# A batched matmul on one core: the last stores on another queue, one of them split, x loaded earlier, transposes moved to their own batch

## The chip, the cores and the metric

The kernel runs on one core of a Trainium2 chip. The metric is the device time of one execution in microseconds (us), lower is better. The first six runs of the kernel before lie within 1.6 us (516.54 to 518.18 us, 0.3%), so differences of about 1 us need several runs, and here they also need the traces.

## The reference

```python
batch, m, k, n = 32, 512, 1024, 768
x:      float32 [32, 512, 1024]
weight: float32 [32, 1024, 768]
return np.matmul(x, weight).astype(np.float32)      # [32, 512, 768]
```

## The kernel before

For every batch, x (2 MB in HBM) and the weights (3 MB) are loaded on POOL's queue and cast to bf16 on the way; PE transposes x with an identity, multiplies, ACT and DVE copy the result out of PSUM, and the output (1.5 MB) is stored as a transfer of 128 partitions with a row of 12,288 bytes each. The last four batches go through their weights in chunks (`CHUNKED`), and in them the transposes of the next batch stand before the last chunk of the current one. Cuts are marked; the comments in the code are mine.

```python
CHUNKED = {B - 4: (4, 4), B - 3: (4, 4), B - 2: (4, 4), B - 1: (4, 2, 2)}
AHEAD = 3
# ... [cut] ...
x_pool = ctx.enter_context(tc.tile_pool(name="x", bufs=4))
# ... [cut] ...
for b in range(1, AHEAD):
    load_x(b)                      # nc.gpsimd.dma_start
    load_w(b)                      # nc.gpsimd.dma_start, one per chunk
ready = {}
for b in range(B):
    if b + AHEAD < B:
        load_x(b + AHEAD)
        load_w(b + AHEAD)
    if b > 0:
        nc.gpsimd.dma_start(out=out_view[b - 1], in_=outs[b - 1])
    outs[b] = out_pool.tile([P, MT * N], F32, name="out_sb")
    # ... [cut: batches that are not chunked] ...
    xT = ready.pop(b, None) or {mt: transpose(b, mt) for mt in range(MT)}
    pms = [banks() for _ in range(2)]
    at = 0
    for n in CHUNKED[b]:
        last = at + n == KT
        for mt in range(MT):
            if last and b + 1 < B:
                ready.setdefault(b + 1, {})[mt] = transpose(b + 1, mt)
            matmuls(pms[mt // 2], mt % 2, xT[mt], b, range(at, at + n), True)
            if last and mt % 2 == 1:
                pair = mt // 2
                evacuate(b, pair, pms[pair])
                if b == B - 1:     # the last output, two halves
                    cols = slice(pair * N2, (pair + 1) * N2)
                    nc.sync.dma_start(out_view[b, :, cols], outs[b][:, cols])
        at += n
```

## Time and profile before

| | before |
|---|---|
| median of the first 3 runs | 516.96 us (516.54 to 517.15) |
| span of the profiled run | 516.0 us |
| HBM traffic | 167.8 MB read, 50.3 MB written, 423 GB/s over the span |
| chain of waits | DMA 88%, PE 9% |

These are lines of the profile page of the kernel before: the DMA queues (packets, megabytes, share of the sixteen engines' span) and the summary of the chain that ended last.

```profile
q0 software_dynamic: 14256, 131.60, 98.9%
q1 hardware_dynamic: 432, 3.67, 1.9%
q8 instruction: 20, 0.33, 0.2%
...
HBM read 167.77 MB, written 50.33 MB: 423 GB/s over the span
...
DMA 88%; PE 9%; issue 1%; DVE 0%; ACT 0%; POOLq 0%
```

Queue 0 is POOL's, queue 1 SP's, and queue 8 brings instructions: 20 packets of 16 KB. The kernel is bound by DMA. The next view is the table by stages of the kernel before, 1 us each, at its end. Its last three columns are the granted TensorE clock, the mean busy share of the DMA engines and the GB/s that they moved.

```profile
core 0: us, PE busy (x) PEld busy (x) DVE busy (x) ACT busy (x) POOL busy (x), PEclk, DMA share, GB/s
505.00:506.00 1.00, 1.00 (x8) 0.59 (x7) 0.00 (x0) 0.00 (x0) 0.00 (x0) 1.00 0.90 381
506.00:507.00 1.00, 1.00 (x8) 0.67 (x7) 0.00 (x0) 0.44 (x1) 0.00 (x0) 1.00 0.60 258
507.00:508.00 1.00, 1.00 (x8) 0.59 (x6) 0.69 (x1) 0.87 (x3) 0.00 (x0) 1.00 0.43 184
508.00:509.00 1.00, 0.54 (x3) 0.10 (x1) 0.64 (x1) 0.83 (x2) 0.00 (x0) 1.00 0.46 190
509.00:510.00 1.00, 0.00 (x0) 0.00 (x0) 0.05 (x1) 0.16 (x1) 0.00 (x0) 1.00 1.01 418
510.00:511.00 1.00, 0.00 (x0) 0.00 (x0) 0.00 (x0) 0.00 (x0) 0.00 (x0) 1.00 1.01 412
511.00:512.00 1.00, 0.00 (x0) 0.00 (x0) 0.00 (x0) 0.00 (x0) 0.00 (x0) 1.00 1.02 418
```

The dip at 506 to 509 us looks like 1.5 us of DMA time lost to waiting for PE. And a store transfer of 128 partitions alone, at a share of 1.01 to 1.02, moves 412 to 418 GB/s; this pair of numbers, share against GB/s, will matter.

Why the dip is not lost time is seen in what the page averages away. The trace has sixteen completion marks for each of these transfers. I read them as one for each DMA engine. For the last weights and the transfers after them in the kernel before, in us:

| transfer | first mark | last mark | last mark after the one before it |
|---|---|---|---|
| last weights of batch 31 | 491.07 | 496.45 | |
| store 27 | 494.88 | 500.12 | 3.67 |
| store 28 | 498.60 | 503.80 | 3.68 |
| store 29 | 502.26 | 507.45 | 3.65 |
| store 30 | 505.91 | 511.11 | 3.66 |
| store 31, first half | 511.00 | 512.97 | 1.86 |
| store 31, second half | 512.89 | 514.80 | 1.83 |

The slowest engine goes on without a hole: every 1.5 MB takes it 3.66 us, the halves 1.85. The others are up to 5.4 us ahead, and the dip is theirs. The lag of the slowest was 0.8 us at 40 us and grew later, among others in steps of 1.1 us near 246 and 440 us; packets of queue 8 ran at 245.2 and 442.8 us.

These lines of the timeline of the kernel before (start, duration, engine, line, instruction, and in brackets the idle time before it and what ended it) show x as the wait of batch 30's last chunk, and when the last stores were issued.

```profile
489.12 0.75 PE L68 MATMUL pt<-ident,x_sb 128*128 128x128 f32 x4 [3.28 <-DMA x_sb<-in_x_dram]
...
499.19 0.53 POOL L130 DMA_DIRECT2D out_dram<-out_sb  x1 [16.95 <-ACT out_sb L112]
...
507.89 1.62 SPq L159 DMA_DIRECT2D out_dram<-out_sb  x2
```

### The profile page before, as it was taken

The page shows a single profiled execution, that of the slowest core. Times are in us where ns is not written, and L with a number is a line of the kernel's source. Part 1 is how long each engine was busy: PE and PEld are TensorE (multiplying, and loading weights), DVE is VectorE, ACT ScalarE, POOL GpSimd, SP SyncE. Part 2 cuts the span into 40 slices and gives each one's busy share as a digit, 9 for nine tenths or more (in the row PEclk, how much of TensorE's full clock was granted, in tenths as well). Part 3 has the DMA queues.
Part 4 walks back from the last instruction along what each step waited for, and adds up shares of the span by engine and source line. Part 5 has one row for each costly group of instructions (what it writes and reads, how often), then busy time and mean ns, then how long its engine had stood idle before and what let it go on. Part 6 is the DMA issues. An engine that isn't in the chain of part 4 may idle for free.

```text
span 516.0 us, 5924 instructions
## 1 busy us (share of the span) xinstructions
PE 426.4 (83%) x2528; PEld 279.6 (54%) x2576; DVE 129.7 (25%) x196; ACT 76.3 (15%) x129; POOL 53.4 (10%) x105
## 2 busy tenths in 40 slices
PE   0999998698887879977798797987878987969794
PEld 0766665465554555654555464654545554646462
DVE  0433333133131231322313232222223132312221
ACT  0111111011111111110111011111111110101111
POOL 3011010100101001100011001010100110111000
PEclk9999999799898997998989799898989898979989
DMA  8999999999999999999999999999999999999996
GB/s 255 218 218 211 215 274 275 272 272 241 255 280 273 275 254 241 276 277 274 267 240 268 274 276 272 247 252 278 275 274 256 247 267 275 276 267 239 259 390 261
DMA packets 14714, 135.65 MB, mean 263 GB/s; under 512 B 1632, under 2 KB 1632, under 8 KB 3040
## 3 DMA queue, kind: packets, MB, share of 16 engines
q0 software_dynamic: 14256, 131.60, 98.9%
q1 hardware_dynamic: 432, 3.67, 1.9%
q8 instruction: 20, 0.33, 0.2%
q14 instruction: 6, 0.05, 0.0%
HBM read 167.77 MB, written 50.33 MB: 423 GB/s over the span
## 4 chain that ended last, share of the span: by engine, by line
DMA 88%; PE 9%; issue 1%; DVE 0%; ACT 0%; POOLq 0%
DMA x_sb<-in_x_dram 37%; DMA w_sb<-in_weight_dram 25%; DMA out_dram<-out_sb 24%; PE pm L99 7%; DMA x_first<-in_x_dram 2%; PE pt L81 1%; PE pt L68 1%; DVE out_sb L111 0%; DVE xT L70 0%; ACT out_sb L112 0%; POOLq L130 0%; POOLq L54 0%; POOLq L60 0%
## 5 line engine op out<-in xcount | busy, mean ns | idle before, releaser
L99 PE MATMUL pm<-w_sb,xT 128*128 128x256 bf16 (+1 forms) x2000 | 370.2, 340 | 60.9 <-DMA w_sb<-in_weight_dram 56.8
L99 PEld LDWEIGHTS <-xT 128*128 128x128 bf16 x2048 | 206.8, 102 | 198.3 <-issue 66.5
L70 DVE COPY xT<-pt 128x1024 bf16<-128x1024 bf16 x124 | 83.0, 689 | 245.4 <-PE pt L68 245.4
L68 PE MATMUL pt<-ident,x_sb 128*128 128x128 f32 x496 | 77.4, 290 | 8.9 <-DMA x_sb<-in_x_dram 8.6
L68 PEld LDWEIGHTS pt<-ident,x_sb 128*128 128x128 f32 x496 | 73.7, 207 | 17.2 <-issue 7.1
L110 ACT COPY out_sb<-pm 128x512 f32<-128x512 f32 x64 | 37.5, 586 | 289.6 <-PE pm L99 280.7
L111 DVE COPY out_sb<-pm 128x512 f32<-128x512 f32 x64 | 43.9, 687 | 115.5 <-PE pm L99 114.8
L112 ACT COPY out_sb<-pm 128x512 f32<-128x512 f32 x64 | 37.5, 586 | 142.5 <-PE pm L99 142.4
L54 POOL DMA_DIRECT2D x_sb<-in_x_dram x31 | 16.5, 533 | 172.8 <-DMA w_sb<-in_weight_dram 141.6
L60 POOL DMA_DIRECT2D w_sb<-in_weight_dram x37 | 19.8, 534 | 132.4 <-DMA out_dram<-out_sb 65.6
L130 POOL DMA_DIRECT2D out_dram<-out_sb x31 | 16.6, 536 | 140.8 <-DMA x_sb<-in_x_dram 62.8
L81 PE MATMUL pt<-ident,x_first 128*128 128x128 f32 x32 | 5.7, 338 | 12.4 <-DMA x_first<-in_x_dram 12.4
L81 PEld LDWEIGHTS pt<-ident,x_first 128*128 128x128 f32 x32 | 4.9, 202 | 13.0 <-issue 12.3
L82 DVE CAST xT<-pt 128x512 bf16<-128x512 f32 x8 | 5.5, 727 | 18.4 <-PE pt L81 18.3
L110 ACT ACT_TABLE_LOAD x1 | 1.3, 1283 | 0.7 <-PEq L175 0.7
masks.py:199 POOL TENSOR_SCALAR_AFFINE_SELECT ident<-ident 128x128 f32<-128x128 f32 x1 | 0.3, 288 | 0.1
masks.py:197 POOL MEMSET ident<- 128x128 f32 x1 | 0.2, 223 | 0.0
L175 POOL MEMSET const-float32-0.0<- 128x1 f32 x1 | 0.1, 99 | 0.2 <-issue 0.2
L175 POOL MEMSET const-bfloat16-1.0<- 128x1 bf16 x1 | 0.1, 102 | 0.0
L175 POOL MEMSET const-uint8-127<- 128x1 uint8 x1 | 0.1, 102 | 0.0
L175 POOL MEMSET const-float32-1.0<- 128x1 f32 x1 | 0.1, 98 | 0.0
## 6 DMA issues: line engine op xcount, KB each, us to landing
out_dram<-out_sb POOLq DMA_DIRECT2D x31, 1536.0 KB, 41.9
w_sb<-in_weight_dram POOLq DMA_DIRECT2D x28, 1536.0 KB, 43.2
x_sb<-in_x_dram POOLq DMA_DIRECT2D x31, 1024.0 KB, 39.6
w_sb<-in_weight_dram POOLq DMA_DIRECT2D x7, 768.0 KB, 32.5
x_first<-in_x_dram SPq DMA_DIRECT2D x1, 2048.0 KB, 11.5
out_dram<-out_sb SPq DMA_DIRECT2D x2, 768.0 KB, 5.3
w_sb<-in_weight_dram POOLq DMA_DIRECT2D x2, 384.0 KB, 28.7
```

The costliest lines, as they stand in the source:

```text
L54: nc.gpsimd.dma_start(out=xs[b], in_=x_view[b])
L60: nc.gpsimd.dma_start(out=ws[b][:, at:at + n, :], in_=w_view[b, :, at:at + n, :])
L68: nc.tensor.transpose(pt[:, j, :], pairs[:, mt, j::JT], ident)
L70: nc.vector.tensor_copy(xT.rearrange("p j m r -> p (j m r)"), pt.bitcast(BF16).rearrange("p j m -> p (j m)"))
L81: nc.tensor.transpose(pt[:, i, :], x_first[:, mt, JT * h + i::KT], ident)
L82: nc.vector.tensor_copy(xT[:, 2 * h:2 * h + 2].rearrange("p j m r -> p j r m"), pt.rearrange("p (j r) m -> p j r m", r=2),)
L99: nc.tensor.matmul(pm[bank][:, at:at + size], xT[:, ko // 2, :, ko % 2], ws[b][:, ko, off:off + size], start=(ko == 0 and not (together an ...
L110: nc.scalar.copy(o[:, 0:512], pm[0])
L111: nc.vector.tensor_copy(o[:, 512:1024], pm[1])
L112: nc.scalar.copy(o[:, 1024:N2], pm[2])
L130: nc.gpsimd.dma_start(out=out_view[b - 1], in_=outs[b - 1])
L175: nc = _bacc.Bacc("TRN2", target_bir_lowering=False, num_devices=1)
```

## The change

The intent: let the last weights and the last matmuls not wait for x (x four batches ahead, transposes in their own batch); let the last stores go on a second queue; and even out the DMA engines' loads by sending 32 partitions of store 29 in four transfers of eight partitions each (every fourth of the 32).

```diff
+    LATE = 4
+    FEW = 32
...
-    x_pool = ctx.enter_context(tc.tile_pool(name="x", bufs=4))
+    x_pool = ctx.enter_context(tc.tile_pool(name="x", bufs=5))
...
+        load_x(AHEAD)
         for b in range(B):
+            if b + AHEAD + 1 < B:
+                load_x(b + AHEAD + 1)
             if b + AHEAD < B:
-                load_x(b + AHEAD)
                 load_w(b + AHEAD)
-            if b > 0:
+            if 0 < b <= B - LATE:
                 nc.gpsimd.dma_start(out=out_view[b - 1], in_=outs[b - 1])
+            if b == B - 1:
+                for late in (B - 2, *range(B - LATE, B - 2)):
+                    first = FEW if late == B - 3 else 0
+                    for at in range(first // 8):
+                        few = slice(at, first, first // 8)
+                        nc.sync.dma_start(out_view[late, few], outs[late][few])
+                    nc.sync.dma_start(out_view[late, first:], outs[late][first:])
...
-            xT = ready.pop(b, None) or {mt: transpose(b, mt) for mt in range(MT)}
+            xT = {0: transpose(b, 0)}
...
-                    if last and b + 1 < B:
-                        ready.setdefault(b + 1, {})[mt] = transpose(b + 1, mt)
+                    if mt + 1 not in xT and mt + 1 < MT:
+                        xT[mt + 1] = transpose(b, mt + 1)
```

More of the change, by code (lines that the diff above doesn't have):

```diff
@@ L122 @@
             load_w(b)
-        ready = {}
+        load_x(AHEAD)
         for b in range(B):
+            if b + AHEAD + 1 < B:
+                load_x(b + AHEAD + 1)
             if b + AHEAD < B:
-                load_x(b + AHEAD)
                 load_w(b + AHEAD)
-            if b > 0:
+            if 0 < b <= B - LATE:
                 nc.gpsimd.dma_start(out=out_view[b - 1], in_=outs[b - 1])
+            if b == B - 1:
[5 more added lines that the diff above has]
+                    nc.sync.dma_start(out_view[late, first:], outs[late][first:])
             outs[b] = out_pool.tile([P, MT * N], F32, name="out_sb")
```

## The prediction

> **What bounds it now.** The chain of waits is 88% DMA. HBM traffic is 218 MB in 516 us, 423 GB/s, and the slices show the DMA engines at 90% or more in all slices but the last. PE waits 57 us for weights (waits view). The sixteen completion marks of each transfer (trace) come 3.66 us apart on the last engine for each 1.5 MB store and 4.86 us for each 2 MB x, without a hole from 100 us on to the end. So one DMA engine is never idle, and its load is the time.
>
> That engine is behind the others: first and last mark of one transfer lie 0.8 us apart at 40 us, 3.3 at 110, 4.4 from 246, 5.4 from 440 (steps of 1.1 us, each when an instruction fetch of 16 KB, 0.9 us, runs). At the end of the last store on POOL's queue the fastest engine finishes at 505.9 us, half of them by 508, the slowest at 511.1. Each half of the last output (768 KB) then costs that engine 1.83 us: 513.0, 514.8; the span ends at 516.0. In 1 us windows the mean DMA share falls to 0.60, 0.43, 0.46 at 506 to 509 us: that is the other engines waiting for PE (last matmuls end at 508.6), not the slowest one.
>
> **What the change does.**
> 1. x one batch earlier: same bytes, in another order. w of batch 30 lands 4.9 us later (481 to 485 us), w of batch 31 as before (496.4). POOL keeps eight transfers in flight (issue to landing about 42 us); x needs the slot of batch b-1 in both kernels. Worth 0.
> 2. Transposes with their own batch: the waits for x inside batches 28 to 30 go (3.3 us at 489). Same count of PE instructions. PE should finish batch 30 at about 494 and batch 31 at about 506, 2 to 3 us earlier. The critical engine is never waiting for PE: worth 0 by itself.
> 3. Stores of 30, 28, 29 on SP's queue from about 494 us, beside what POOL's queue still holds. Same bytes and, by the trace, the same rate (SP's 768 KB in 1.83 us, POOL's 1.5 MB in 3.66). The slowest engine has POOL work until 500, so no hole. Worth 0.
> 4. The split of store 29: the only part that alters the critical engine's load. [...] So the low eight carry 4+6 rows in place of 8, the high eight 6. A 12,288 B row is 0.46 us (packet times in the trace): the high eight are relieved by 0.92 us, the low eight get 0.92 more. The trace doesn't name engines; I take it (about 75%) that the slowest is one of the high eight. Then the end comes 0.9 us earlier; otherwise up to 0.9 later.
>
> **Predicted: 516.1 us, 515.0 to 517.4.** Faster by over 2%: 1%; within 2%: 98%; slower: 1%.
>
> **What would show it.** Right: last completion mark 0.9 us earlier; PE's last matmul near 506; no dip in DMA share between 500 and 510; no waits for x in batches 30 and 31. Steps 1 to 3 wrong: last marks not 3.66/4.86 us apart, or a POOL wait for a buffer.
>
> **What would make it wrong.** The slowest engine among the low eight; two queues at once moving more or less than one does; SP's stores issued after 500 us because batch 30 ends late; the spread growing differently with the new order; PE throttled at the end (0.5 clock at 490 to 493).

"Low eight" is here and below only a name for the eight engines that run the transfers of eight partitions, and "lowest four" one for those that run the transfers of four: the traces number no engines. That the four transfers of eight would meet the same eight engines, and the 96 partitions all sixteen, was my estimate. The runs show it: in the trace of the kernel after, each transfer of eight has eight marks behind the one at its issue, and the one of 96 partitions has sixteen (507.59 to 512.19 us); in e12_sp_few the engines part into two groups of eight, up to 39 us apart. That transfers of four meet the same four engines each time, and that these are among the low eight, was not shown. (The first slice of the page, too, is below 90%, at 8 tenths.)

## The result

| | before | after |
|---|---|---|
| median | 516.94 us (516.54 to 518.18, 6 runs) | 518.24 us (517.42 to 519.39, 6 runs) |
| ratio | | 1.0023, 95% interval 1.0008 to 1.0039 |

A ratio is the mean time of one kernel's fast runs over that of the other's of the same rounds, so it is not quite the ratio of the medians. The kernel became slower by about 1.3 us, within 2% but outside the predicted range.

The answering lines of the profile page after:

```profile
q0 software_dynamic: 13824, 126.88, 96.3%
q1 hardware_dynamic: 896, 8.39, 4.2%
q8 instruction: 20, 0.33, 0.2%
...
HBM read 167.77 MB, written 50.33 MB: 421 GB/s over the span
...
DMA 83%; PE 13%; issue 1%; DVE 1%; ACT 0%; POOL 0%; POOLq 0%
```

The same bytes moved, 4.7 MB of them from queue 0 to queue 1. The timeline after, with the wait for the weights that replaced the one for x, and SP's issues:

```profile
481.07 2.72 PE L101 MATMUL pm<-w_sb,xT 128*128 128x512 bf16 x8 [3.38 <-DMA w_sb<-in_weight_dram]
...
494.50 2.21 SPq L140 DMA_DIRECT2D out_dram<-out_sb  x2
496.76 5.50 SPq L139 DMA_DIRECT2D out_dram<-out_sb  x4
502.30 1.22 SPq L140 DMA_DIRECT2D out_dram<-out_sb  x1
505.99 2.81 SPq L169 DMA_DIRECT2D out_dram<-out_sb  x2
```

The schedule came out as meant: batch 30 no longer waits for x, SP issues stores 30 and 28 at 494.5 us, the four transfers of eight at 496.8, the other 96 partitions at 502.3, and the last output at 506.0, 1.9 us earlier than before. The table by stages after:

```profile
core 0: us, PE busy (x) PEld busy (x) DVE busy (x) ACT busy (x) POOL busy (x), PEclk, DMA share, GB/s
505.00:506.00 1.00, 1.00 (x9) 0.61 (x7) 0.69 (x1) 0.87 (x3) 0.00 (x0) 1.00 1.12 356
506.00:507.00 1.00, 0.64 (x4) 0.13 (x2) 0.54 (x1) 0.83 (x2) 0.00 (x0) 1.00 0.96 320
507.00:508.00 1.00, 0.00 (x0) 0.00 (x0) 0.15 (x1) 0.26 (x1) 0.00 (x0) 1.00 0.95 307
508.00:509.00 1.00, 0.00 (x0) 0.00 (x0) 0.00 (x0) 0.00 (x0) 0.00 (x0) 1.00 0.90 350
509.00:510.00 1.00, 0.00 (x0) 0.00 (x0) 0.00 (x0) 0.00 (x0) 0.00 (x0) 1.00 1.06 399
510.00:511.00 1.00, 0.00 (x0) 0.00 (x0) 0.00 (x0) 0.00 (x0) 0.00 (x0) 1.00 1.04 406
```

The dip at 506 to 509 us is filled: from 505 to 511 us the share is 0.90 or more (the slice at 503 us has 0.79). But at that share the engines move 307 to 356 GB/s at 505 to 509 us, where a 128-partition store alone in the kernel before (509 to 512 us) moved 412 to 418. Busy DMA engines were not engines at their rate here. By the marks, that is the time in which most engines run the transfer of 96 partitions (its marks come at 507.59 to 512.19 us).

The completion marks after show where the last engine's time went. Store 28's last mark is at 506.63 us; that of the last transfer of eight at 508.47 (1.84 us for four rows, as a row of 0.46 us says); that of the 96 partitions at 512.19 (3.72 us for this engine's six rows, of which 2.76 would be due); then 514.04 and 515.88 for the halves. The rows of that engine took 0.46, 0.46, 0.46, 0.69, 0.53 and 1.12 us. Since its marks are among those of the transfers of eight, it is one of the low eight engines, the ones that got more rows. It was so already before the split: store 28's last mark is followed by the last mark of the first transfer of eight after 0.47 us, one row, and in the two other traces of this kernel after 0.46 and 0.47.

To compare traces without the scatter of the earlier part, I use three pieces: the last mark of batch 31's weights (POOL's 95th transfer in the new order), the tail from there to the last mark of all, and the end of the program behind it.

| trace | weights' last mark | tail | end | span |
|---|---|---|---|---|
| before, two traces | 496.45, 496.75 | 18.35, 18.39 | 1.17, 1.15 | 515.96, 516.28 |
| after, three traces | 495.63, 495.10, 495.76 | 20.25, 19.64, 19.27 | 1.74, 1.73, 1.74 | 517.62, 516.47, 516.77 |

The second and third traces come from runs told below. The tail is longer by 0.9 to 1.9 us, and the end by 0.57. In the end of after, SP checks six further semaphores of its own transfers after the last mark (0.37 us, up to 516.30 us in the first trace), the ten transfers on SP having used eight of them, two twice; in before, with three transfers and three semaphores, it checks none after its last.

### The profile page after: what moved, and what is told of

It reads as the page before. It is cut to its first block, busy times and chain, and to the rows that moved or that the text cites. A ratio compares the mean times of both kernels' runs of the same rounds, so it can differ in the third digit from the quotient of the medians.

```text
span 517.6 us, 5981 instructions
## 1 busy us (share of the span) xinstructions
PE 427.5 (83%) x2576; PEld 278.5 (54%) x2576; DVE 129.8 (25%) x196; ACT 76.2 (15%) x129; POOL 51.7 (10%) x102
## 4 chain that ended last, share of the span: by engine, by line
DMA 83%; PE 13%; issue 1%; DVE 1%; ACT 0%; POOL 0%; POOLq 0%
DMA w_sb<-in_weight_dram 48%; DMA out_dram<-out_sb 25%; PE pm L101 12%; DMA x_sb<-in_x_dram 8%; DMA x_first<-in_x_dram 2%; PE pt L83 1%; PE pt L70 1%; DVE out_sb L113 0%; DVE xT L72 0%; ACT out_sb L114 0%; POOL w_sb L62 0%; POOLq L133 0%; POOLq L62 0%; POOLq L56 0%
## 5 line engine op out<-in xcount | busy, mean ns | idle before, releaser
L70 PE MATMUL pt<-ident,x_sb 128*128 128x128 f32 x496 | 75.1, 285 | 0.0
L133 POOL DMA_DIRECT2D out_dram<-out_sb x28 | 15.0, 536 | 119.4 <-DMA x_sb<-in_x_dram 67.0
## 6 DMA issues: line engine op xcount, KB each, us to landing
out_dram<-out_sb POOLq DMA_DIRECT2D x28, 1536.0 KB, 41.9
```

The lines of the kernel that those rows point to most:

```text
L70: nc.tensor.transpose(pt[:, j, :], pairs[:, mt, j::JT], ident)
```

## The experiments

Theory S: the split costs, because the slowest engine is among the low eight and because the rows of the 96-partition transfer were slow. Rival Q: the second queue, the earlier x or the moved transposes cost.

### e1_nosplit: the change without the split

```diff
-    FEW = 32
+    FEW = 0
```

> The changed kernel with store 29 in one transfer of 128 partitions (no eight-partition transfers). Theory S (the split is what costs: the slowest DMA engine is one of the low eight and gets 10 rows instead of 8 of store 29, 0.92 us, and its six rows of the 96-partition transfer took 3.7 us instead of 2.8, 0.96 us more): about 1.9 us less than the changed kernel, so about 516.3 us, ratio to before about 0.9985, last completion mark near 514.0 us. Rival Q (stores on a second queue beside POOL's, the earlier x or the moved transposes cost the time): about 518.2, ratio about 1.002, as the changed kernel.

Measured: 517.13 us (516.80 to 517.56, 5 runs), ratio 1.0004, interval 0.9993 to 1.0016; tail 18.39 us. So the split accounts for the loss: without it the change is worth nothing, and rival Q falls. (The two intervals overlap a little, 1.0008 to 1.0016, and the ranges of the times by 0.1 us; the runs below carry the point further.) The time is 0.8 us above the expected 516.3; I had expected the earlier mark of the weights in the first trace (495.63 against 496.45) to be a gain of the new order, and the untraced times don't show it.

### e2_even: 32 and 96 partitions, even rows

```diff
-                    for at in range(first // 8):
-                        few = slice(at, first, first // 8)
-                        nc.sync.dma_start(out_view[late, few], outs[late][few])
+                    if first:
+                        nc.sync.dma_start(out_view[late, :first], outs[late][:first])
```

> The changed kernel with the 32 partitions in one transfer of 32 (2 rows on each of 16 engines) and the other 96 as they are (6 rows each): no engine gets more rows than another. If the slow rows belong to the 96-partition transfer itself: about 1.0 us above the kernel without a split, 517.3 us, and rows of 12,288 B that take 0.5 to 1.2 us instead of 0.46 are seen in the trace. If only the number of rows counts and the slow rows were an accident: as the kernel without a split, 516.3. Rival Q: 518.2.

Measured: 518.01 us (517.60 to 520.58, 6 runs), ratio 1.0028 (1.0012 to 1.0043); tail 19.05. With no engine getting more rows than another (the view of the DMA issues gives both parts a landing, 12.3 and 13.4 us after the issue, as it does only for transfers with sixteen marks), 0.9 us of the loss is still there in the times, 0.7 in the trace. In the times this kernel is no faster than the changed one (1.0023), so they show no cost of the unequal rows; that cost is read from the marks alone.

### e3_twice: store 28 split as well

```diff
-                    first = FEW if late == B - 3 else 0
+                    first = FEW if late != B - 2 else 0
```

> The changed kernel with store 28 split as store 29 is: the suspected cost doubled. Theory S: 1.9 us more than the changed kernel, about 520.1 us, ratio to before about 1.006. Rival Q: as the changed kernel, 518.2.

Measured: 520.00 us (518.70 to 521.67), ratio 1.0061 (1.0043 to 1.0078), where theory S expected 520.1; tail 20.47. The dose follows, but this run doubles both suspected costs at once, so it doesn't part them.

### e4_fours: transfers of four partitions

```diff
+                    nc.sync.dma_start(out_view[late, first:], outs[late][first:])
-                    for at in range(first // 8):
-                        few = slice(at, first, first // 8)
+                    for at in range(first // 4):
+                        few = slice(at, first, first // 4)
                         nc.sync.dma_start(out_view[late, few], outs[late][few])
-                    nc.sync.dma_start(out_view[late, first:], outs[late][first:])
```

> The changed kernel with the 32 partitions in eight transfers of four, put behind the 96-partition transfer on SP's queue: [...] It tells which engine is the slowest. If the slowest is among the lowest four: 6 rows more than in the kernel without a split (2.8 us) and the slow rows (1.0 us): about 520 us. If it is the fifth to the eighth: 2 rows less (0.9) and the slow rows: about 516.4, and the completion marks of the four-partition transfers all come before the slowest engine's. Rival Q: 518.2 in both.

Measured: 519.72 us (519.10 to 520.81), ratio 1.0053 (1.0040 to 1.0066). As a time it tells nothing of the slowest engine, because I had overlooked how long SP would be held. SP's timeline of this run:

```profile
500.48 11.72 SPq L140 DMA_DIRECT2D out_dram<-out_sb  x8
512.32 0.84 SPq L169 DMA_DIRECT2D out_dram<-out_sb  x2
```

Eight small transfers held SP for 11.7 us, and the last output was issued at 512.3 us instead of 506.0. Not all of it is issuing: the first four took 1.23 to 1.27 us each, but the last started only at 511.62 us, when the 96-partition transfer, whose semaphore it uses again, had landed (511.61). Its marks do tell something: the four marks of each transfer of four lie within 0.2 us of each other, while the slowest engine finished the 96-partition transfer 2.97 us after the first. So in this trace the slowest is not among the four engines that finished these transfers.

### e5_cols: cut by columns

```diff
+                    cut = N if first else 0
+                    if first:
+                        nc.sync.dma_start(out_view[late, :, :cut], outs[late][:, :cut])
+                    nc.sync.dma_start(out_view[late, :, cut:], outs[late][:, cut:])
```

(These replace the transfers of eight and the one of 96 partitions.)

> The changed kernel with store 29 cut by columns instead of partitions: two transfers of 128 partitions, 3,072 and 9,216 B of each row, the same bytes and the same number of transfers as in the run with 32 and 96 partitions. If it is the 96-partition shape that makes rows slow: as the kernel without a split, 517.1 us, and no slow rows in the trace. If a further transfer in the tail is what costs: about 518.0, as the run with 32 and 96 partitions.

Measured: 517.06 us (516.75 to 517.13), ratio 0.9994 (0.9982 to 1.0006); tail 18.43. A further transfer of 128 partitions in the tail costs nothing that is seen (517.06 us against 517.13 in e1_nosplit); leaving the 128-partition shape does (518.01 in e2_even). The table by stages of this run, at the same place:

```profile
507.00:508.00 1.00, 0.00 (x0) 0.00 (x0) 0.09 (x1) 0.20 (x1) 0.00 (x0) 1.00 1.04 430
508.00:509.00 1.00, 0.00 (x0) 0.00 (x0) 0.00 (x0) 0.00 (x0) 0.00 (x0) 1.00 0.98 406
509.00:510.00 1.00, 0.00 (x0) 0.00 (x0) 0.00 (x0) 0.00 (x0) 0.00 (x0) 1.00 1.02 424
```

406 to 430 GB/s at a share of 0.98 to 1.04, against 307 and 350 at 0.95 and 0.90 in the changed kernel at 507 to 509 us.

### e6_low8, e7_low4, e8_before_low4: load moved in the middle of the kernel

A quarter of the columns of store 20 goes on SP's queue, in transfers of eight partitions (e6_low8) or four (e7_low4), on the changed kernel without the split; e8_before_low4 does the latter on the kernel before. Theory L says that the load of the slowest engine sets the time, rival T that only the tail or the 96-partition shape counts. The quarter takes 24,576 B, two rows, from each engine's share of POOL's transfer; that the transfers of four would all pass by the slowest engine, and so relieve it by 0.92 us, was my estimate.

```diff
-                nc.gpsimd.dma_start(out=out_view[b - 1], in_=outs[b - 1])
+                cut = N if b - 1 == MOVED else 0      # MOVED = 20
+                nc.gpsimd.dma_start(out=out_view[b - 1, :, cut:], in_=outs[b - 1][:, cut:])
+                for start in range(0, P if cut else 0, 32):
+                    for at in range(start, start + 32 // 8):          # e7, e8: 32 // 4
+                        few = slice(at, start + 32, 32 // 8)          # e7, e8: 32 // 4
+                        nc.sync.dma_start(out_view[b - 1, few, :cut], outs[b - 1][few, :cut])
```

> The changed kernel without the split at the end; instead a quarter of the columns of store 20, in the middle of the kernel, goes on SP's queue in sixteen transfers of eight partitions: the lowest eight engines carry 24,576 B (2 rows) more, the others as much less, as in the change, but without a 96-partition transfer and far from the end. Theory L (the time is the load of the slowest engine, which is one of the low eight): 0.9 us more than the kernel without a split, about 518.0. Rival T (only what happens in the tail or the 96-partition shape counts): 517.1.

> The same with 32 transfers of four partitions: [...] Theory L: 0.9 us less than the kernel without a split, about 516.2 us, ratio to before about 0.9986; the last completion marks of the twelve others come 0.9 us earlier. Rival T: 517.1.

> The kernel before with the same 32 transfers of four partitions for a quarter of store 20 and nothing else changed. Theory L: 0.9 us less than before, about 516.0 us, ratio about 0.998. Rival T: as before, 516.9.

Measured: e6_low8 516.23 us, ratio 0.9988 (0.9974 to 1.0002); e7_low4 517.46, ratio 1.0003 (0.9990 to 1.0016); e8_before_low4 518.24, ratio 1.0016 (1.0004 to 1.0028). All three times go against theory L as I had it, with the slowest engine always in the low eight; e7_low4's is near the 517.1 of rival T, the two others fit neither. The six runs of e6_low8 fall into two groups: 515.94, 516.15, 516.20, 516.25 and 517.66, 517.79.

### e9_sp to e12_sp_few: the suspects taken 31 times

All 31 whole stores of the kernel before go on SP's queue, in parts as named (`PARTS` stands for them in the diff): whole (e9_sp), as 32 and 96 partitions (e10_sp_96), as 64 and 64 (e11_sp_64), and as four transfers of eight and one of 96 (e12_sp_few).

```diff
-                nc.gpsimd.dma_start(out=out_view[b - 1], in_=outs[b - 1])
+                for part in PARTS:
+                    nc.sync.dma_start(out_view[b - 1, part], outs[b - 1][part])
```

> The kernel before with all 31 whole stores on SP's queue, each one transfer of 128 partitions, so beside POOL's loads instead of among them. It is the base of the next three runs, and a test of rival Q thirty times as large as the change: if a store costs more for running on a second queue, this is slower than before by thirty times that; if not, 516.9 us within 0.6.

> As the run with all stores on SP's queue, but every store in two transfers, of partitions 0 to 31 and 32 to 127: no engine gets more rows than another. The suspected cost of the shape taken 31 times. If the 96-partition shape slows the rows as it did at the end (0.6 to 1.0 us a store): 19 to 30 us more than that run, about 536 to 547 us. If it does so only when no loads run beside it: less than 3 us more.

> The same with every store in two transfers of 64 partitions. If only the 128-partition shape keeps the rate: slower than the run with 128 by 10 us or more. If 96 is the special case (its rows in sixes): as the run with 128, 516.9 us.

> The same with every store split as the change splits store 29: 32 partitions in four transfers of eight, and 96. If the lowest eight engines carry 2 rows more of each such store, and the busiest engine's load sets the time (theory L): 31 times 0.92 us, 28 us, more than the run with 32 and 96 partitions. If the four transfers of eight are spread evenly after all, or load on one engine does not set the time: as the run with 32 and 96 partitions.

| run | median us | ratio to before, interval |
|---|---|---|
| e9_sp | 524.86 | 1.0154 (1.0112 to 1.0196) |
| e10_sp_96 | 523.59 | 1.0119 (1.0101 to 1.0136) |
| e11_sp_64 | 523.60 | 1.0123 (1.0100 to 1.0147) |
| e12_sp_few | 556.37 | 1.0754 (1.0718 to 1.0790) |

e12_sp_few against e10_sp_96 is 32.8 us for 31 stores, 1.06 us each, where 0.92 was worked out from two rows: the transfers of eight do load eight engines and always the same ones, and the load of the busiest engine sets the time. In its trace the sixteen marks of a POOL transfer fall into two groups of eight, up to 39 us apart. Theory L, in this general form, is shown.

e10_sp_96 and e11_sp_64 are not slower than e9_sp: beside loads, no cost of these shapes is seen (each kernel's runs scatter by 2 to 5 us). In the table by stages of e10_sp_96, the middle of the kernel moves the 262 GB/s at a share of 1.02 that the kernel before moves there (263 at 1.02); e9_sp has 262 at 1.02 too, so the second queue costs nothing there either:

```profile
200.00:300.00 100.00, 82.20 (x487) 53.80 (x495) 25.70 (x39) 14.65 (x25) 6.86 (x13) 0.93 1.02 262
```

e9_sp itself is a miss: I expected 516.9. Its table by stages shows where its time goes:

```profile
500.00:510.00 10.00, 9.95 (x64) 6.41 (x63) 3.34 (x5) 1.76 (x3) 0.00 (x0) 1.00 0.91 288
510.00:520.00 10.00, 5.11 (x31) 2.94 (x30) 1.38 (x2) 2.30 (x4) 0.00 (x0) 0.89 0.40 163
```

On a queue of their own the stores no longer stand behind the loads, so they finish early (13.8 us from issue to landing in the median, against 41.9 in before) and the last weights late (last mark at 507.9 us, against 496.4); then nothing is left to move while PE does the last batch (share 0.40 at 510 to 520 us). In before and after, stores 27 to 30 cover that work (share 1.02 at 500 to 505 us in before).

### e13_even3 and e14_halves3: the shape in the tail

The kernel of e2_even with all three late stores split, as 32 and 96 or as 64 and 64 partitions.

```diff
-                    first = FEW if late == B - 3 else 0
+                    first = FEW              # e14_halves3: 2 * FEW
```

> All three late stores (30, 28, 29) split into 32 and 96 partitions, even rows on all engines. If the 96-partition transfer is slow when no loads run beside it (0.9 us for the one in the earlier run): up to 2.7 us above the kernel without a split, about 519 to 519.8 us; the first of them still meets POOL's last loads and may cost less. If the 0.9 us came from elsewhere: as the run with one such split, 518.0, or less.

> The same three stores as two transfers of 64 partitions each, same number of transfers. If the 96-partition shape alone is slow: about 517.2. If every shape but 128 partitions is slow: about 519 or more.

Measured: e13_even3 521.76 us (520.26 to 524.10), ratio 1.0103 (1.0069 to 1.0138), tail 21.81; e14_halves3 525.52 us (522.25 to 526.08), ratio 1.0151 (1.0118 to 1.0183), tail 23.05. The first is above what I expected (519 to 519.8), the second within its "519 or more". 96 is not special: 64 and 64 is as bad or worse (the ranges overlap). The table by stages of e14_halves3:

```profile
508.00:509.00 1.00, 0.00 (x0) 0.00 (x0) 0.00 (x0) 0.00 (x0) 0.00 (x0) 1.00 1.03 350
509.00:510.00 1.00, 0.00 (x0) 0.00 (x0) 0.00 (x0) 0.00 (x0) 0.00 (x0) 1.00 1.15 313
510.00:511.00 1.00, 0.00 (x0) 0.00 (x0) 0.00 (x0) 0.00 (x0) 0.00 (x0) 0.58 0.84 301
```

Again busy engines with few bytes. In the packet records, the same can be counted for the 12,288-byte rows on SP's queue that ended after POOL's last packet:

| trace | such rows | of these over 500 ns |
|---|---|---|
| e1_nosplit | 202 | 0 |
| e5_cols | 132 | 0 |
| e9_sp | 100 | 0 |
| after, three traces | 256, 289, 283 | 41, 38, 36 |
| e2_even | 184 | 45 |
| e13_even3 | 313 | 120 |
| e14_halves3 | 276 | 75 |
| e10_sp_96 | 128 | 67 |
| e11_sp_64 | 128 | 109 |

Whole 128-partition stores have none. Every trace listed with a transfer of 96 or 64 partitions in the tail has dozens. And one trace shows the condition: in e10_sp_96, of the 3,840 rows on SP's queue before POOL's last packet, 3 took over 500 ns (in e11_sp_64, 2).

### e15_after_again and e16_low8_again: is it always the same engine that is slowest?

I read the packets of queue 8 as taking turns over eight engines, each with a duration of its own. In order the durations are 893, 893, 948, 945, 935, 974, 974 and 961 ns (within a few ns in most traces), round and round, but the first one differs between traces. The 20 packets of a run give the first four three turns and the others two. In e12_sp_few, whose order starts with 935, the marks of the first four turns grow late within the eight engines that carry fewer rows; I read from this that the engines of 935 to 961 are in the high eight and those of 893 to 945 in the low. (There the durations are a little shorter: 935, 960, 961, 954.) Theory R: which engines come first decides whether more load on the low eight harms.

The kernels are unchanged.

> The changed kernel once more, for another trace of it. Theory R: [...] the first one of a run is not fixed; the four that come first get three of the 20 fetches, about 1.1 us each, and are the slowest. The split helps or harms by 0.9 us according to whether those four are in the high or the low eight. If this run's fetches start with durations other than 893, 892, 948, 945 ns, namely with 935, 974, 974, 961: about 517.5 to 518.1 us, not 519.4. If they start as in the first trace: about 519.4. Against R: the same start and a time below 518.3, or the other start and 519 or more.

> The kernel with a quarter of store 20 in transfers of eight, once more; its six runs fell into two groups, 515.9 to 516.3 and 517.7 to 517.8 us, and the traced one of the fast group started its fetches with 935, 974, 974, 961 ns. Theory R: that start again: 515.9 to 516.4; start with 893, 892, 948, 945: 517.5 to 518. Against R: the reverse.

Measured, one run each, state unknown: e15_after_again started with 893 and took 518.26 us, against R by the letter of the expectation (I had said 519.4). e16_low8_again started with 893 and took 518.78 us, on the side that R expects, 0.8 us further than it said.

The traces are sharper than the times. From the last mark of POOL's 61st transfer (near 341 us) to that of the last weights, the slowest engine took, in the traces of the new order:

| trace | first turn | stretch, us |
|---|---|---|
| after (three), e1_nosplit, e2_even, e3_twice, e5_cols, e14_halves3 | 893, 935, 948, 974 | 154.41 to 154.45 |
| e13_even3 | 893 | 154.59 |
| e4_fours (no load moved here either) | 893 | 156.64 |
| e6_low8 (low eight loaded) | 935 | 153.79 |
| e16_low8_again (the same kernel) | 893 | 155.31 |
| e7_low4 (lowest four loaded, the others relieved) | 893 | 153.52 |

The same kernel lost 0.88 us or gained 0.64 us in this stretch, with another turn of the fetches, and e7_low4 gained 0.91, where 0.92 was expected. That the turn is the cause is not shown by these few traces: e4_fours lost 2.2 us with no load moved, and its trace has 65 packets of POOL's queue over 1 us between 340 and 440 us where after has 2; e16_low8_again has 15 of them, e6_low8 1. The gain of e7_low4 is missing from its times. Its trace, the slowest of its five runs, was late before store 20 was touched (342.64 us at POOL's 61st transfer, where the others have 340.7 to 341.9), but that says nothing of the other four. Why, is open; e8_before_low4, whose order of transfers is the other one, can't be put into this table, and its loss of 1.2 us stays open but for the end of its program, 1.87 us against 1.17.

### e17_before_again and e18_after_third

The kernels are unchanged.

> The kernel before once more, for a second trace. In all traces without a split the last completion mark comes 18.3 to 18.4 us after the last mark of the last weights, and this should again be so; what differs is when the weights land (496.45 us in the first trace of before, 495.1 to 496.2 in the kernels with the new order). If the new order of x and stores gained about 0.8 us that the split hid: 496.2 to 496.7 again. If it is scatter from run to run (then the new order is worth nothing, as its median without a split says): the mark can lie anywhere from 495 to 496.5, and the time 516.4 to 517.7 follows it.

> The changed kernel, a third trace. From the last mark of the last weights to the last mark of all took 20.25 and 19.63 us in two traces, 18.3 to 18.4 without a split, 19.06 with even rows. Theory S: again 19 to 20.3, and the end of the program 1.7 us behind the last mark (1.2 in before). If the fetches start with 935 or 974 ns (the slowest in the high eight): near 19.0; if with 893: 19.6 or more.

Measured, one run each, state unknown: e17_before_again 518.05 us, e18_after_third 518.54 us; another run of before beside them took 516.34. The tail of before is 18.39 us again, and the weights' last mark is at 496.75, so nine of the ten traces of the new order in which no load was moved before this mark (495.1 to 496.2) are earlier than both of before; the tenth, e4_fours, is later (497.87). In the medians this gain does not appear (e1_nosplit 517.13 against 516.94); whether the new order is worth up to 1 us stays open. The third trace of the changed kernel started with 893 and has a tail of 19.27 us: theory S holds (19 to 20.3, end 1.74), but not the finer claim that this start gives 19.6 or more. The varying part is in the slow rows.

## Why the prediction was wrong

The prediction's base held. DMA bounds the kernel, the slowest engine has no hole, and steps 1 to 3 (earlier x, transposes, stores on SP's queue) were worth nothing together: 517.13 us without the split, ratio 1.0004. PE ended at about 506 us as predicted, and the dip in the DMA share went without a gain, as predicted.

The step that failed is number 4, "the split of store 29": it counted rows at one price and forecast a gain of 0.92 us for the slowest engine, where that engine got rows more and the transfer that the split leaves over ran slower. Three terms were wrong.

- "The slowest is one of the high eight (about 75%)". In all three traces of the changed kernel the engine with the last marks is one of the low eight, which got 10 rows of store 29 in place of 8. There I had no evidence, only the thought that the split must have been made to help. In other traces the slowest may be on the other side: e6_low8 gained, e16_low8_again lost, with another first turn of the instruction fetches. If so, the split aims at an engine that does not stay put; two traces don't show it.
- "A 12,288 B row is 0.46 us." That is true of 128-partition transfers and of the transfers of eight; it is wrong of the 96-partition transfer that the split leaves over, when no loads run beside it: 36 to 41 rows of 0.5 to 1.45 us in the three traces. With even rows this alone makes the tail 0.7 us longer in the trace (19.05 against 18.39) and the median 0.9 us (518.01 against 517.13).
- The end of the program was not in the sum: 1.74 us after the last mark instead of 1.17, by the checks of SP's further transfers (0.37) and a longer end on POOL (0.67 us from its clearing of the semaphores to its last drain, against 0.20), less 0.28 us by which POOL began sooner after SP (0.03 us against 0.30). e1_nosplit and e2_even have 1.35 and 1.36.

"Otherwise up to 0.9 later" was thus the row count alone. On the slowest engine the marks add up: two rows more (0.92) in each of the three traces, and on top 0.96, 0.36 and 0.00 us of slow rows (its six rows of the 96 took 3.72, 3.12 and 2.75 us where 2.76 was due). That makes the 1.9, 1.3 and 0.9 us by which the tails exceed the 18.37 of before, mean 1.4. With 0.57 for the end, 1.9 us is expected of the traced runs, against 1.3 measured in the medians; the difference is the earlier mark of the weights in the new order, or runs with another turn, and I can't part the two. How much of the measured loss is the row count stays open as well: e2_even, without it, has the same time as the change.

Why a transfer of 96 or 64 partitions is slow by itself was not tested, and the traces, which have no addresses, do not show it.

None of the experiments beats the kernel before clearly. e6_low8 (0.9988, interval to 1.0002) comes nearest, and its gain may hang on the turn of the fetches.

## What to carry to other kernels

In this kernel, which DMA bounds, the busiest of the sixteen engines set the end, not the mean share: in e12_sp_few, two rows more on eight of them in each of 31 stores cost 32.8 us. So read the sixteen completion marks of a transfer, and before shifting load to even them out, take several traces to see whether the slowest engine is the same in each (the same shift of load gained 0.64 us or lost 0.88 in two traces here). Keep transfers at 128 partitions at the end, where no loads run beside them, and cut by columns if they must be cut: one late store cut by columns took 517.06 us and whole 517.13, but as 32 and 96 partitions 518.01, and three of them as 32 and 96 took 521.76, as 64 and 64 525.52. Where a stage has full DMA share and fewer GB/s than another stage with the same kind of transfer, as here 307 to 356 against 412 to 418, its transfers are slow. The kind matters: the middle of this kernel, with its casting loads, has 263 GB/s at a share of 1.02, because the page counts a load after the cast (x with 1,024 KB, of 2 MB in HBM).

## Further measurements

- With no loads beside them, the stages with stores of 96 or 64 partitions shown above moved 301 to 356 GB/s at a share of 0.84 to 1.15, those with 128 partitions 406 to 430 at 0.98 to 1.04. Beside this kernel's loads no cost was seen (3 slow rows of 3,840 before POOL's last packet, 67 of 128 after, in e10_sp_96).
- Four transfers of eight in each of 31 stores cost 32.8 us and parted the engines into two fixed groups of eight (e12_sp_few). The traces don't number the engines.
- 20 packets of queue 8, of 16 KB and 0.89 to 0.98 us each, ran beside the transfers, read here as turns over eight engines, with a step of about 1.1 us in the lag of the slowest engine at two of them. Whose instructions they bring, the traces don't tell.
- Here the lag can't be put down to fixed engines: the same kernel lost 0.88 us or gained 0.64 us by the same shift of load in two traces (the first with slow packets of its own, as told above).
- An issue on SP's queue took 0.33 to 0.34 us for each half of the last output in before, 1.31 to 1.36 for each transfer of eight in after, about 0.63 for most of e12_sp_few. Size alone does not set it: in after, whole store 30 took 0.34 us and whole store 28 1.82.
- The semaphore checks at the end took 0.37 us for six in after. The end of the program behind the last mark grew from 1.17 us in before to 1.74 with seven more transfers on SP's queue.
